# A hybrid attention and convolution layer on one core: the differences of the weight blocks on GpSimd from pair 23 of the first half on, and two more low halves on VectorE

## The chip, the cores and the metric

The kernel runs on one core of one Trainium2 chip. The core has five engines with queues of their own: TensorE (PE; its weight loads are PEld), VectorE (DVE), ScalarE (ACT), GpSimd (POOL) and SyncE (SP), which here only issues DMAs. Each engine does its queue in order and waits on semaphores for the others. The metric is the device time of one execution in microseconds.

## The reference

One layer with two token mixers, for a prompt of 2048 tokens and for 8 sample tokens, all in float32 (D = 1024; the input projection has 8704 columns):

```python
mod = c @ w_c + b_c;  shift, scale, gate = split(mod, 3)
z = (x * (1 + scale) + shift) @ w_in + b_in
q, k, v, ga, glu, gb, ma, mb = split(z)
# A: dilated causal window attention, 3 groups x 4 heads, combined over the groups by softmax of lse
a = (o_attn * silu(ga)) @ w_pa
# B: GLU, causal depthwise conv of width 31, LayerNorm over channels, swish
b = (conv_out * silu(gb)) @ w_pb
y = (sigmoid(ma) * a + sigmoid(mb) * b) @ w_o
x_out = layer_norm(ALPHA * x + gate * y)
# sample tokens: the same, with attention over caches and a kept conv state
```

The change lies in the weights of `w_in`, in the product that gives `z`.

## The kernel before

**Tiles and stages.** A product in float32 accuracy is made of three passes of a reduced form (float32r): each operand X is split into a high part H, ScalarE's copy of X in that form, and a low part L = X - H, and H·H + L·H + H·L is summed in PSUM. The product with `w_in` goes over two halves of the tokens (`p` 0 and 1) and, in each, over 34 pairs of column blocks of 128 columns. A pair with its 2 x 2 blocks (two blocks of the sum index, `e`, by two column blocks, `x`) is done by Strassen's scheme in Winograd's form: seven products for eight, with the operands b11, b21, T2, T1, T3, b22, T4 from the weights, where T1 to T4 are differences of blocks. In the first half each of the seven goes over two sets of 258 columns, in the second over 512 at once. The function `quad(s, ...)` issues the seven products of pair `s` in a fixed order, into the PSUM banks X, Z, Y and W. Of those, W and Y are single: VectorE must have emptied a bank (`out_of`, line L80, into a staging tile `zst`) before the next product starts there; X and Z are emptied by ScalarE (L568, L579, L589).

**The weights.** `w_raw` loads blocks into tiles `raw` and `rawb` (128 partitions x 512 numbers, 256 KB) over SP's queue. `w_make(s, n)` makes operand `n` of pair `s`. Its `split(r)` takes one of seven buffers `bop`, has ScalarE copy the high part (L238) and GpSimd or VectorE subtract for the low part (L247); a counter gives two of seven low halves to VectorE, by its steps T1 and T4. In the first half the differences are made too: `sub` (L76 on VectorE) makes T1's block with b21, T2's block (`t`) and T4's block with T2, and T3's block with T1; each of them is stored to DRAM (`tw_d`) for the second half, which only loads and splits them. `MAKE` says at which of a pair's 14 steps each operand is made: six products ahead of its first use, b11 and b21 at steps 8 and 9 of the pair before, T2 at 11, T1 at 13, then T3, b22 and T4 at 0, 3 and 5.

**What sets the order.** Everything is issued by one program in the order of the text; each engine's queue is the order of issue. Between products `tick()` lets lanes of other work go on: attention, convolution, normalisation (`conv_norm`), the sample attention (`s_attn`) and the preparation of the second half (`prep_second`). It keeps a planner's clock for TensorE and one for VectorE: every operation on VectorE adds its cost to `clock["dve"]` by `cost`, about 0.68 us for 512 columns, and a lane goes on only while VectorE's clock is less than 0.5 us ahead of TensorE's. A low half on GpSimd is booked at 0.3 us. `later` puts off stores by 2.6 us of the planner's clock.

**Pairs 23 to 33** are the second pair of the convolution's gate, two pairs of the attention's gate and eight pairs of merge gates. While they run, the lanes do the sample attention (products of caches with a query on VectorE, `y<-y,stg`, each followed by a sum), the normalisation of the first half's convolution (statistics on VectorE, three small operations on `lnm` on GpSimd at L772, L773, L834, then ScalarE at L835) and the preparation of the second half. GpSimd also copies two columns of each staged tile (`samples_of`, L615).

Of the kernel before, what the change touches and what calls it, by code (L numbers as in the profile page):

```python
# [11 lines left out]
OP = mybir.AluOpType  # L12
# [29 lines left out]
def f32(ap):  # L42
    return ap.bitcast(F32)
# [3 lines left out]
def hybrid_layer(ctx: ExitStack, tc: tile.TileContext, I, O):  # L47
    nc = tc.nc
    ctx.enter_context(tc.manual_schedule())
    PE, ACT, DVE, POOL = nc.tensor, nc.scalar, nc.vector, nc.gpsimd  # L50

    def ld(out, in_):
        nc.sync.dma_start(out, in_)
# [5 lines left out]
    clock = {"pe": 0.0, "dve": 0.0, "conv": 0.0}  # L59

    def cost(ap, per=1.2, fix=70):
        n = 1
        for s in ap.shape[1:]:
            n *= s
        clock["dve"] += (fix + per * n) / 1000.0
# [8 lines left out]
    def vtt(out, a, b, op):  # L74
        cost(out)
        DVE.tensor_tensor(out, a, b, op=op)  # L76
# [15 lines left out]
    def later(fn, delay=2.6):  # L92

        post.append((clock["pe"] + delay, fn))
# [89 lines left out]
    stream = [(p, n) for p in range(2) for n in range(len(quads[p]))]  # L184
# [47 lines left out]
    split_no = [0]  # L232
    on_dve = [2]

    def w_make(s, n):
        def split(r):
            t = bops[s, n] = bp.tile([P, 2, 4, P], F32R, name="bop", tag="bop", bufs=nbop[0])
            ACT.activation(t[:, 0], r, AF.Copy)  # L238
            split_no[0] += on_dve[0]
            eng = POOL  # L240
            if split_no[0] >= 7:
                split_no[0] -= 7
                eng = DVE
                cost(r)
            else:
                clock["dve"] += 0.3
            eng.tensor_tensor(t[:, 1], r, f32(t[:, 0]), op=OP.subtract)  # L247

        if stream[s][0]:
            split(raws.pop((s, n)) if n[0] == "T" else raws.pop((s, int(n[1]) - 1, int(n[2]) - 1)))  # L250
            return

        def sub(out, a, b, keep):
            vtt(out, a, b, OP.subtract)
            later(lambda: ld(tw_d[stream[s][1], T_OF[keep]].rearrange("p (k n) -> p k n", n=P), out))

        R = lambda e, x: raws[s, e, x]
        if n == "b11":
            split(R(0, 0))
        elif n == "b21":  # L260
            split(R(1, 0))
            sub(R(0, 0), R(0, 1), R(0, 0), "T1")
        elif n == "T2":
            t2 = wp.tile([P, 4, P], F32, name="t2", tag="t2")
            sub(t2, R(1, 1), R(0, 0), "T2")
            split(t2)
            sub(R(1, 0), R(1, 0), t2, "T4")
        elif n == "T1":
            split(R(0, 0))
            sub(R(0, 1), R(1, 1), R(0, 1), "T3")  # L270
        elif n == "T3":
            split(R(0, 1))
        elif n == "b22":
            split(R(1, 1))
        else:
            split(R(1, 0))
            for k in [k for k in raws if k[0] == s]:
                raws.pop(k)
# [1253 lines left out]
    s = 0  # L1532
    for p in range(2):
        state["p"] = p
        cv = None
        for n, pair in enumerate(quads[p]):
            kind, a, b = pair[0]
# [305 lines left out]
```

## Time and profile before

| | us |
|---|---|
| median of 3 runs | 2201.32 (2198.42 to 2202.17) |
| the profiled execution | 2199.83 |
| its span | 2198.0 |
| TensorE busy | 2104.3 |
| VectorE busy | 1343.4 |
| GpSimd busy | 922.4 |
| ScalarE busy | 910.8 |

The first half of the tokens runs to about 925 us, the second from there to about 1780, and the output stage behind it. A view of lines or a timeline names the engine, the line of the code, the operation and its tiles as out<-in; an arrow in brackets names what ended the engine's wait just before. Times are microseconds from the span's start, the mean of one instruction in a group is in nanoseconds.

### The profile page before, as it was taken

How to read it: one execution, taken by the hardware profiler on the slowest of the kernel's cores; microseconds unless marked ns; L12 is line 12 of the kernel's file. 1: busy time of each engine (PE TensorE's matmuls, PEld its weight loads, DVE VectorE, ACT ScalarE, POOL GpSimd, SP SyncE). 2: the span in 40 equal slices, each digit the busy share in tenths (PEclk: the TensorE clock that was granted, in tenths of full speed). 3: DMA queues.
4: the chain of work that ended last, by engine and by line, in shares of the span. 5: the costliest groups of instructions: out<-in, count | busy, mean ns of one | idle time of the engine just before them, and what ended most of it. 6: DMA issues, size and time to landing. Idle time of an engine off the chain costs nothing.

```text
span 2198.0 us, 36412 instructions
## 1 busy us (share of the span) xinstructions
PE 2104.3 (96%) x13185; PEld 1859.5 (85%) x13185; DVE 1343.4 (61%) x2142; ACT 910.8 (41%) x2042; POOL 922.4 (42%) x943
## 2 busy tenths in 40 slices
PE   7799999999998899989999999999999988999998
PEld 3799999999998868968888888888888868888886
DVE  4667676777767733554676767634467826545455
ACT  3424444444444545534444444456555532111110
POOL 2455454444644432454444444445333446232332
PEclk9899999999999999999999999999999999999999
DMA  8265455556669765435554556567898866343320
GB/s 263 91 179 186 139 188 162 159 152 186 186 199 289 222 212 177 159 111 148 166 164 157 180 163 190 189 183 236 264 307 260 269 208 221 115 127 104 99 97 31
DMA packets 404046, 392.09 MB, mean 178 GB/s; under 512 B 26585, under 2 KB 331277, under 8 KB 402833
## 3 DMA queue, kind: packets, MB, share of 16 engines
q1 hardware_dynamic: 336277, 342.63, 50.4%
q10 hardware_dynamic: 67588, 47.13, 6.7%
q8 instruction: 104, 1.70, 0.3%
q14 instruction: 77, 0.63, 0.1%
HBM read 245.91 MB, written 144.29 MB: 178 GB/s over the span
## 4 chain that ended last, share of the span: by engine, by line
PE 52%; DVE 3%; DMA 2%; issue 2%; POOL 2%; ACT 1%; SPq 0%; POOLq 0%; DVEq 0%; ACTq 0%
PE ps_X L498 9%; PE ps_Z L498 9%; PE ps_W L498 9%; PE py L1783 7%; PE pab L1727 5%; PE ps_Y L498 5%; PE ps_S L1225 3%; PE ps_U L1265 1%; PE ps_S L1250 1%; DVE yL L76 1%; PE ps_S L653 1%; PE ps_U L1263 1%; DVE xr L80 1%; DVE st L1666 0%; DVE th L76 0%
## 5 line engine op out<-in xcount | busy, mean ns | idle before, releaser
L247 POOL TENSOR_TENSOR bop<-raw,bop 128x512 fp32r<-128x512 f32 x341 | 487.3, 1434 | 569.9 <-ACT bop L238 467.6
L498 PE MATMUL ps_W<-As,bop 128*128 128x258 f32 (+1 forms) x2448 | 437.6, 327 | 14.6 <-DVE zst L80 12.6
L498 PEld LDWEIGHTS ps_W<-As,bop 128*128 128x128 f32 x2448 | 359.8, 191 | 56.0 <-DVE zst L80 15.5
L80 DVE SCALAR_TENSOR_TENSOR y<-u,cwT,y 128x1024 f32<-128x1024 f32 x240 | 357.6, 1490 | 1.8
L238 ACT ACTIVATE bop<-raw 128x512 fp32r<-128x512 f32 x409 | 251.7, 624 | 77.4 <-DVE raw L76 26.4
L498 PE MATMUL ps_X<-As,bop 128*128 128x258 f32 (+1 forms) x1224 | 221.6, 328 | 10.0 <-ACT c L568 7.0
L498 PE MATMUL ps_Z<-As,bop 128*128 128x258 f32 (+1 forms) x1224 | 223.6, 328 | 2.2 <-ACT c L568 2.2
L498 PE MATMUL ps_X<-Aa,bop 128*128 128x258 f32 (+1 forms) x1224 | 219.0, 328 | 4.0 <-ACT bop L238 1.6
L498 PE MATMUL ps_Y<-Aa,bop 128*128 128x258 f32 (+1 forms) x1224 | 217.8, 325 | 0.6 <-POOL Aa L388 0.6
L498 PE MATMUL ps_Z<-Aa,bop 128*128 128x258 f32 (+1 forms) x1224 | 215.5, 324 | 0.0
L498 PEld LDWEIGHTS ps_X<-As,bop 128*128 128x128 f32 x1224 | 180.4, 192 | 30.0 <-ACT c L568 7.2
L498 PEld LDWEIGHTS ps_X<-Aa,bop 128*128 128x128 f32 x1224 | 182.3, 192 | 24.5 <-ACT bop L238 2.7
L498 PEld LDWEIGHTS ps_Z<-As,bop 128*128 128x128 f32 x1224 | 179.4, 190 | 22.0 <-ACT c L568 2.6
L498 PEld LDWEIGHTS ps_Z<-Aa,bop 128*128 128x128 f32 x1224 | 180.1, 190 | 17.5 <-issue 0.8
L498 PEld LDWEIGHTS ps_Y<-Aa,bop 128*128 128x128 f32 x1224 | 178.0, 189 | 19.1 <-issue 1.8
L1242 ACT ACTIVATE X<-X,mz 128x128 f32<-128x128 f32 (+1 forms) x192 | 87.0, 455 | 167.2 <-DVE mz L84 162.1
L80 DVE SCALAR_TENSOR_TENSOR zst<-ps_W,bT,c 128x258 f32<-128x258 f32 (+1 forms) x102 | 58.4, 573 | 133.7 <-ACT c L589 122.0
L247 DVE TENSOR_TENSOR bop<-raw,bop 128x512 fp32r<-128x512 f32 x68 | 51.9, 764 | 94.4 <-ACT bop L238 90.9
L80 DVE SCALAR_TENSOR_TENSOR X<-ps_S,tabh 128x512 f32<-128x512 f32 (+1 forms) x80 | 52.5, 657 | 81.9 <-PE ps_S L1225 75.6
L80 DVE SCALAR_TENSOR_TENSOR zst<-ps_Y,bT,c 128x258 f32<-128x258 f32 (+1 forms) x90 | 51.5, 572 | 79.3 <-PE ps_Y L498 55.2
L1680 ACT ACTIVATE xr<-xr,lnm 128x1024 f32<-128x1024 f32 (+1 forms) x16 | 19.9, 1244 | 184.0 <-POOL lnm L1679 184.0
L1727 PE MATMUL pab<-oH,wc0H 128*128 128x256 f32 (+1 forms) x256 | 74.3, 290 | 19.7 <-DVE ev L80 17.4
(312 smaller groups left out, 3792.4 us busy)
## 6 DMA issues: line engine op xcount, KB each, us to landing
raw<-w_in SPq DMA_DIRECT2D x205, 256.0 KB
raw<-tw_d SPq DMA_DIRECT2D x136, 256.0 KB
tw_d<-raw SPq DMA_DIRECT2D x102, 256.0 KB
tw_d<-t SPq DMA_DIRECT2D x34, 256.0 KB
rawb<-w_in SPq DMA_DIRECT2D x33, 256.0 KB
wc<-w_c SPq DMA_DIRECT2D x16, 512.0 KB
aq<-zq SPq DMA_DIRECT2D x16, 512.0 KB
xr<-x_prompt SPq DMA_DIRECT2D x16, 512.0 KB
```

The costliest lines, as they stand in the source:

```text
L76: DVE.tensor_tensor(out, a, b, op=op)
L80: DVE.scalar_tensor_tensor(out, a, s, b, op0=op0, op1=op1)
L238: ACT.activation(t[:, 0], r, AF.Copy)
L247: eng.tensor_tensor(t[:, 1], r, f32(t[:, 0]), op=OP.subtract)
L498: PE.matmul(acc[:, :n], w[:, i, b, :], a[:, b, off:off + n], start=start and b == 0 and x == 0, stop=b == 3 and x == 2, skip_group_check=True)
L653: PE.transpose(pt[:, i * P:(i + 1) * P], t[:, i * P:(i + 1) * P], ident)
L1225: PE.matmul(S[:, s:s + w, :], q_of(b), k_of(b, w), start=True, stop=True)
L1242: ACT.activation(X[:, s:s + w, :], X[:, s:s + w, :], AF.Exp, bias=mz[:, n, 0:1], accum_out=mz[:, n, 1:2])
L1250: PE.transpose(pt[:, s, :], X[:, s, :], ident)
L1263: PE.matmul(U[:, n, :], Y[:, s, :], v_of(b, 1), start=True, stop=False)
L1727: PE.matmul(p[:, :n], a, b[:, kt, :n], start=i == 0, stop=i == 11)
L1783: PE.matmul(py[h], a[:, d, c0:c0 + P], w[:, h * 512:(h + 1) * 512], start=f, stop=l)
```

## The change

From pair 23 on, in the first half alone, `sub` puts a difference on GpSimd and books 0.3 us of VectorE's clock for it, and the counter in `split` goes up by four instead of two, so that four of a pair's seven low halves go to VectorE. With the counter where it stands at pair 23 these are b21, T1, b22 and T4; b11, T2 and T3 stay on GpSimd.

```diff
@@ w_make / split
-            split_no[0] += on_dve[0]
+            split_no[0] += on_dve[0] + (2 if stream[s][0] == 0 and s >= 23 else 0)
             eng = POOL
             if split_no[0] >= 7:
                 split_no[0] -= 7
...
@@ w_make / sub
         def sub(out, a, b, keep):
-            vtt(out, a, b, OP.subtract)
+            if s < 23:
+                vtt(out, a, b, OP.subtract)
+            else:
+                clock["dve"] += 0.3
+                POOL.tensor_tensor(out, a, b, op=OP.subtract)
             later(lambda: ld(tw_d[stream[s][1], T_OF[keep]].rearrange("p (k n) -> p k n", n=P), out))
```

In numbers of instructions, 44 differences (four for each of 11 pairs) go from VectorE to GpSimd and 22 low halves from GpSimd to VectorE. Lines behind 258 stand four higher in the changed kernel.

VectorE's queue where pair 23's operands b21, T2, T1, T3 and b22 are made, before: `raw<-raw` is T1's difference, made with b21, `t_7897<-rawb,raw` and `raw<-raw,t_7897` are T2's and T4's, `raw<-rawb,raw` is T3's; `bop<-raw,bop` is a low half, `zst<-ps_...` the emptying of a bank.

```order
L80 SCALAR_TENSOR_TENSOR zst<-ps_W,bT,u_7688 128x258
L76 TENSOR_TENSOR raw<-raw 128x512
L80 SCALAR_TENSOR_TENSOR zst<-zst 128x256
L76 TENSOR_TENSOR t_7897<-rawb,raw 128x512
L76 TENSOR_TENSOR raw<-raw,t_7897 128x512
L80 SCALAR_TENSOR_TENSOR zst<-zst 128x256
L80 SCALAR_TENSOR_TENSOR zst<-ps_W,bT,c_7944 128x258
L247 TENSOR_TENSOR bop<-raw,bop 128x512
L76 TENSOR_TENSOR raw<-rawb,raw 128x512
L80 SCALAR_TENSOR_TENSOR zst<-zst 128x256
```

The same place of VectorE's queue in the changed kernel, up to b22's low half (`bop<-rawb,bop`):

```order
L80 SCALAR_TENSOR_TENSOR zst<-ps_W,bT,u_7688 128x258
L247 TENSOR_TENSOR bop<-raw,bop 128x512
L80 SCALAR_TENSOR_TENSOR zst<-zst 128x256 x2
L80 SCALAR_TENSOR_TENSOR zst<-ps_W,bT,c_7944 128x258
L247 TENSOR_TENSOR bop<-raw,bop 128x512
L80 SCALAR_TENSOR_TENSOR zst<-zst 128x256
L80 SCALAR_TENSOR_TENSOR ysS<-ysS,ps_S 128x8 x4
L80 SCALAR_TENSOR_TENSOR zst<-ps_Y,bT,c_7970 128x258
L80 SCALAR_TENSOR_TENSOR zst<-ps_W,bT,u_7877 128x258
L80 SCALAR_TENSOR_TENSOR zst<-zst 128x256
L247 TENSOR_TENSOR bop<-rawb,bop 128x512
```

b21's low half stands where the first difference stood; the two differences of T2's step and that of T1's step are gone from between the emptyings of W; b22's low half has come in three steps later.

GpSimd's queue for the same operands, before (`sgb<-zst` are the copied columns of staged tiles):

```order
L247 TENSOR_TENSOR bop<-raw,bop 128x512
L615 COPY sgb<-zst 128x2
L247 TENSOR_TENSOR bop<-raw,bop 128x512
L615 COPY sgb<-zst 128x2
L247 TENSOR_TENSOR bop<-t_7897,bop 128x512
L615 COPY sgb<-zst 128x2
L247 TENSOR_TENSOR bop<-raw,bop 128x512
L615 COPY sgb<-zst 128x2 x2
L247 TENSOR_TENSOR bop<-rawb,bop 128x512
```

And in the changed kernel, where the differences have the line L258:

```order
L247 TENSOR_TENSOR bop<-raw,bop 128x512
L619 COPY sgb<-zst 128x2
L258 TENSOR_TENSOR raw<-raw 128x512
L619 COPY sgb<-zst 128x2
L258 TENSOR_TENSOR t_7897<-rawb,raw 128x512
L247 TENSOR_TENSOR bop<-t_7897,bop 128x512
L258 TENSOR_TENSOR raw<-raw,t_7897 128x512
L619 COPY sgb<-zst 128x2
L258 TENSOR_TENSOR raw<-rawb,raw 128x512
L247 TENSOR_TENSOR bop<-raw,bop 128x512
L619 COPY sgb<-zst 128x2 x5
```

T2's step is now three operations of 128 x 512 in a row on GpSimd, with T3's difference and low half behind them, and nothing of that size follows in the pair until T4 has been made and the next pair begins.

## Rows read from the trace of the kernel before

**Rows 1.** Page, first part: busy us (share of the span) and instructions by engine.
```profile
PE 2104.3 (96%) x13185; PEld 1859.5 (85%) x13185; DVE 1343.4 (61%) x2142; ACT 910.8 (41%) x2042; POOL 922.4 (42%) x943
```

**Rows 2.** Stretches: us, busy PE, PEld, DVE, ACT, POOL, then PEclk, DMA share, GB/s.
```profile
500.00:660.00 160.00, 160.00 (x1312) 158.37 (x1312) 107.89 (x162) 72.09 (x177) 77.85 (x97) 1.00 0.63 194
660.00:770.00 110.00, 98.06 (x759) 94.30 (x758) 84.56 (x149) 56.32 (x127) 48.56 (x71) 0.97 0.82 255
770.00:925.00 155.00, 151.26 (x1094) 130.28 (x1093) 60.66 (x116) 78.23 (x179) 49.90 (x84) 0.99 0.61 190
```

**Rows 3.** Waits of TensorE, 660 to 925: total us, times, longest.
```profile
PE ps_W L498 <- DVE zst L80: 7.1, 8, 2.6
PE ps_Z L498 <- ACT c L568: 2.2, 2, 1.3
```

**Rows 4.** Timeline of TensorE, rows behind a wait: start, us; in brackets the wait.
```profile
664.81 1.85 PE L498 MATMUL ps_W<-As,bop 128*128 128x258 f32 x12 [2.58 <-DVE zst L80]
...
700.59 1.70 PE L498 MATMUL ps_W<-As,bop 128*128 128x258 f32 x12 [1.03 <-DVE zst L80]
...
732.30 0.55 PE L896 MATMUL ps_S<-ident,y 128*128 128x128 f32 x3 [1.31 <-ACT y L835]
747.43 2.40 PE L498 MATMUL ps_W<-As,bop 128*128 128x258 f32 x12 [2.06 <-DVE zst L80]
...
781.05 0.31 PE L983 MATMUL ps_S<-ident,y 32*128 32x32 f32 x3 [1.55 <-DVE y L72]
781.75 2.57 PE L498 MATMUL ps_W<-As,bop 128*128 128x258 f32 x12 [0.39 <-DVE zst L80]
840.30 0.24 PE L1009 MATMUL ps_S<-ident,y 32*128 32x32 f32 x1 [1.34 <-DVE y L80]
```

**Rows 5.** Stretches around two standstills, for the granted clock (PEclk).
```profile
672.00:747.40 75.40, 67.96 (x543) 65.21 (x542) 61.67 (x112) 39.27 (x89) 33.57 (x50) 1.00 0.86 264
747.40:753.00 5.60, 5.57 (x33) 5.57 (x34) 3.98 (x7) 2.37 (x5) 2.04 (x4) 0.70 1.01 300
...
781.70:787.00 5.30, 5.10 (x29) 4.80 (x30) 1.85 (x7) 3.80 (x10) 3.23 (x11) 0.68 1.01 310
```

**Rows 6.** Timeline of VectorE at 664, 739 to 744 and 838.
```profile
664.27 0.49 DVE L80 SCALAR_TENSOR_TENSOR zst<-ps_W,bT,u 128x258 f32<-128x258 f32 x1 [4.44 <-DMA sb_d<-zst]
...
739.06 0.69 DVE L76 TENSOR_TENSOR raw<-raw 128x512 f32<-128x512 f32 x1 [2.47 <-POOL bop L247]
...
743.21 0.67 DVE L76 TENSOR_TENSOR t<-rawb,raw 128x512 f32<-128x512 f32 x1
...
743.97 0.69 DVE L76 TENSOR_TENSOR raw<-raw,t 128x512 f32<-128x512 f32 x1
...
838.18 0.69 DVE L76 TENSOR_TENSOR raw<-raw 128x512 f32<-128x512 f32 x1 [1.51 <-POOL bop L247]
```

**Rows 7.** Lines, 660 to 925: busy us, mean ns | idle before, what ended it.
```profile
L247 DVE TENSOR_TENSOR bop<-raw,bop 128x512 fp32r<-128x512 f32 x20 | 13.9, 694 | 47.3 <-ACT bop L238 47.3
...
L76 DVE TENSOR_TENSOR u<-u,y 128x256 f32<-128x256 f32 x16 | 11.1, 697 | 0.5
...
L76 DVE TENSOR_TENSOR raw<-raw 128x512 f32<-128x512 f32 x10 | 6.9, 688 | 7.5 <-POOL bop L247 7.5
...
L238 ACT ACTIVATE bop<-t 128x512 fp32r<-128x512 f32 x10 | 6.3, 631 | 6.3 <-DVE t L76 4.8 <-ACT smg L609 1.1 <-DVE raw L76 0.2
```

**Rows 8.** Timeline of GpSimd and VectorE at 711 and 765.
```profile
711.82 1.29 POOL L247 TENSOR_TENSOR bop<-raw,bop 128x512 fp32r<-128x512 f32 x1 [0.81 <-ACT bop L238]
711.92 1.47 DVE L76 TENSOR_TENSOR u<-u,y 128x256 f32<-128x256 f32 x1
...
765.88 0.42 DVE L76 TENSOR_TENSOR u<-u,y 128x256 f32<-128x256 f32 x1
```

**Rows 9.** Waits of SP's queue, 660 to 925.
```profile
SPq L53 <- DVE raw L76: 31.8, 11, 8.9
```

**Rows 10.** Lines, 660 to 925: ScalarE's normalisation.
```profile
L835 ACT ACTIVATE y<-ps_S,lnm 128x512 f32<-128x512 f32 x8 | 6.2, 776 | 4.2 <-POOL lnm L834 2.3 <-POOL lnm L772 0.7 <-ACT smg L609 0.6
```

## The prediction

> **What bounds the kernel now.** The first view is the page's busy table: TensorE works for 2104.3 of 2198.0 us [rows 1], so another engine's load matters only where TensorE stands still for it. The second is the table of stretches. The change touches the weight splits of the pairs 23 to 33, which are made between about 660 us (the first moved difference starts right behind the first row of [rows 6]) and the end of the first half, at 925. Before that stretch, from 500 to 660, TensorE is busy all the time although VectorE is busy for 67% of it. From 660 to 770 TensorE is busy for 98.06 of 110 us and VectorE for 77%; from 770 to 925 TensorE for 151.26 of 155 and VectorE for 39% [rows 2]. So some 15.7 us of standstill lie in the part that changes, 11.9 of them in the first 110 us, where the dot products of the sample attention, the gates and the convolution's normalisation share VectorE with the weights.
>
> The third view, the waits of TensorE in that part, says who ended them: 7.1 us went by before a product into bank W while VectorE had still to empty it, 2.2 us before a product into Z for ScalarE's copy of X or Z [rows 3]; the timeline names the large ones singly [rows 4]. Then there is the clock. The granted clock is at its upper level, 2.4 GHz (1.00), through 672 to 747.4 although that holds a standstill of 1.31 us at 732.30. It is a mix of both levels, 0.70 and 0.68 on the mean, in the 5.6 us from 747.4 and the 5.3 us from 781.7 [rows 5], right behind the standstills of 2.06 us and of 1.55 and 0.39 us together. Each such stretch loses 5.6 x 0.30 = 5.3 x 0.32 = 1.7 us.
>
> **What the change removes.** Per pair VectorE gives away four differences and takes two more low halves: b21 and b22, beside T1 and T4 that it had. In the order of its queue b21's low half takes the very place of b21's difference (the second row of both pieces of VectorE's order above), so there nothing is won but a wait that changes its name: the difference waited for GpSimd's split, 7.5 us in 10 [rows 7]; the low half will wait for ScalarE's copy, which is what ends GpSimd's split too. At 838.18 the difference came after a wait of 1.51 us [rows 6] and the standstill at 840.30 stands behind it; ScalarE's copy for b21 ends there at about the same time, so I leave those 1.34 us in. What really leaves the queue are T2's two differences in a row and T3's one; b22's low half is new, at a place with no difference before.
>
> Sum over 11 pairs: 44 differences at 0.69 us are 30.4 us (the timeline's 0.69 and 0.67 [rows 6]), 22 low halves at 13.9 / 20 = 0.69 us [rows 7] are 15.3; VectorE is relieved by 15 us, 6% of 265 us.
>
> What of it TensorE gets, standstill by standstill [rows 4]. At 664.81 nothing: VectorE itself stood 4.44 us for a store of a staging tile [rows 6], before the first changed instruction. At 747.43: between 743.21 and bank W's emptying VectorE ran T2's differences, 0.67 and 0.69 us [rows 6]; without them 2.06 becomes 0.7, worth 1.4. At 781.05 and 781.75: T3's difference, 0.69, stands ahead of the chain of the softmax; 1.55 becomes 0.9 and 0.39 goes, worth 1.0. At 700.59 the same 0.69 of 1.03 goes, worth 0.7. The remaining four of the eight standstills for bank W are 7.1 - 2.58 - 1.03 - 2.06 - 0.39 = 1.0 us together; I take half, 0.5. Sum 3.6 us. With them the two low stretches of the clock should go, since both standstills end below the 1.31 us that left the clock alone: 3.4 us.
>
> **What it adds.** GpSimd runs a difference in 1.29 us (its own split of the same size [rows 8]) against 0.69. Per pair GpSimd has five operations of this size now and seven then: 9.0 us for 6.5, in a pair of 265 / 11 = 24 us, with its load at 98 of 265 us now [rows 2]. So it does not become the bound by load. Every split is made six products, some 10 us at 1.70 each [rows 4], ahead of its use, and the split's chain (a difference, ScalarE's copy of 0.63 us [rows 7], a low half) is 3.2 us, so no product should wait for a weight. Who waits in the new order: ScalarE's copy of T2 and of T3's block stands behind a GpSimd difference, 0.6 us longer, 22 x 0.6 = 13 us at most, on an engine that is half idle [rows 2]; behind the copy stand its copies of the banks X and Z. That could cost from nothing to the whole 2.2 us over again [rows 3]; I take half, 1.1. The stores of the differences stand on SP's queue, which already waits 31.8 us for VectorE's differences [rows 9]; the loads and stores behind them will start 0.6 to 2 us later, and the weights' loads have a whole pair of lead, so I take nothing. GpSimd's three small operations of a normalisation now can stand behind more differences: ScalarE's normalisation waited for them 3.0 us in all over eight cases [rows 10], and one of these waits became the 1.31 us at 732.30 [rows 4]; I take one more of that size, 1.3. The planner books less for VectorE, so the sample attention and the normalisation come up to ten products sooner; the same work is done, and behind pair 33 the order is word for word what it was, so I take nothing for it but the scatter in the range.
>
> **The sum.** 3.6 + 3.4 - 1.1 - 1.3 = 4.6 us gained. The profiled execution took 2199.83 us, 1.8 us of it outside its span and 1.5 us under the median of the runs; taken off the median, 2201.32 becomes 2196.7.
>
> **The port.** At 711.82 GpSimd subtracts until 713.11, and VectorE's product of two tiles in SBUF, begun at 711.92, takes 1.47 us and ends 0.3 us behind it; undisturbed it takes 0.42 [rows 8]. Over the part, 16 of these took 0.697 us each [rows 7]: 16 x 0.28 = 4.4 us of blocking. The new order puts GpSimd's differences right beside VectorE's low halves for b21 and T1, 22 times. The Trainium skill, "SBUF — State Buffer", section "Who interferes with whom", says that a VectorE instruction with two SBUF inputs and a GpSimd instruction that reads SBUF exclude each other, the later one standing until the other is through; the row of 711.92 agrees with that. By that rule both the old differences and the new low halves pay, and GpSimd's longer hold speaks against the change.
>
> **Rivals.** First, the relief is eaten (no change). With 22 low halves meeting a GpSimd difference for half its length, 22 x 0.65 = 14 us, VectorE's 15 us are gone; GpSimd's seven operations for five raise the 4.4 us of blocking to 6.2. Then only half of the 3.6 us comes and one of two low clock stretches stays: 1.8 + 1.7 - 2.4 = 1.1 us gained, 2200.2. For it: the low halves that now go to VectorE were hardly disturbed (0.694 on the mean [rows 7]) because both engines wait for the same copies, which ends here. Against it: the places that cost most, 743 to 744 and 776, lose their VectorE work altogether.
>
> Second, GpSimd's queue becomes the late one (slower). At T2 it now runs difference, low half and difference, and at T3 another difference: four operations, 5.2 of 24 us, where it ran two. Of eight normalisations 8 x 5.2 / 24 = 1.7 fall there; one that stands behind two operations waits 2.6 us, and ScalarE, which does things in order, holds back its copy of X or Z. Now such waiting, 3.0 us in all, gave 1.31 us of standstill; 2.5 us would be one like 747.43, with the clock's 1.7 behind it: 1.7 x 4.2 = 7.1 us. With the first rival's small gain, 7.1 - 1.1 = 6.0 us lost, 2207.3. It decides from two such standstills on. For it: VectorE's statistics come without regard to GpSimd. Against it: GpSimd is idle for 60% of the part and catches up within a pair.
>
> **How the numbers follow.** A run of this kernel can tell about 0.2%, 4.4 us, from no change. My forecast, 2196.7, lies just beyond it: 0.45 for faster. The best case takes all of VectorE's own share, 7.1 - 2.58 + 1.55 + 1.34 = 7.4 us, and both clock stretches, 3.4, at no cost: 2190.5. The eaten relief and its neighbourhood has 0.38, the late GpSimd queue 0.17. The forecast's own range is 2190.5 to 2199; for eight in ten it must reach over the second case and up to the edge of the third: 2190.5 to 2206.
>
> **What would show it.** Right: TensorE's wait for VectorE before bank W falls from 7.1 us to about 4 in 660 to 925, no standstill of 2 us behind 670, the granted clock 1.00 from 672 on to 925, and the stretch before 925 ends 4 to 5 us sooner. Port rival: VectorE's low halves grow well over 0.69 us, those on `raw` to 1.0 or more, and its busy time hardly falls. GpSimd rival: ScalarE waits longer for `lnm` and for GpSimd's differences, and new standstills end with ScalarE. What would make me wrong altogether is a standstill of over 2 us at a place that has none now, brought by the sample work that comes at other times.

## The result, and the profile after

The changed kernel took 2213.71 us (median; 2211.65 to 2214.71) against 2200.99 for the kernel before: a ratio of 1.0058, 95% interval [1.0046, 1.0069]. It is slower by 12.7 us, where 4.6 us of gain were forecast, and it lies above the range. The profiled execution of after took 2214.71 us, its span is 2212.9.

The first part of the page of after, busy us and share of the span, answers to [rows 1]:

```profile
PE 2108.4 (95%) x13185; PEld 1865.7 (84%) x13185; DVE 1335.1 (60%) x2120; ACT 910.3 (41%) x2042; POOL 947.2 (43%) x965
```

TensorE's busy time has hardly moved (2104.3 before). Load went from VectorE (8 us less) to GpSimd (25 us more), as the change says. So the lost time is TensorE's standstill, and the stretches of after (columns as in [rows 2]) say where:

```profile
660.00:770.00 110.00, 87.65 (x656) 85.07 (x655) 75.61 (x135) 50.95 (x114) 53.41 (x75) 0.91 0.84 256
770.00:925.00 155.00, 148.91 (x1082) 127.52 (x1081) 59.29 (x103) 76.46 (x176) 61.80 (x93) 1.00 0.55 176
```

From 660 to 770 TensorE works 87.65 us, where it worked 98.06, though VectorE is busy for 9 us less there. The place where both kernels go on alike is found with a landmark: near the end of the first half stands a wait of 3.00 us for bank W that both kernels have. TensorE's timeline, first of before, then of after:

```profile
934.91 2.21 PE L498 MATMUL ps_W<-As,bop 128*128 128x258 f32 x12 [3.00 <-DVE zst L80]
```

```profile
948.38 2.52 PE L502 MATMUL ps_W<-As,bop 128*128 128x258 f32 x12 [3.00 <-DVE zst L80]
```

The same work ends 13.5 us later, so 13.5 of the 14.9 us between the two profiled spans lie ahead of it, and what follows gives nothing back. One stretch from 645 to that landmark, first of before, then of after:

```profile
645.00:934.80 289.80, 271.23 (x2031) 246.28 (x2029) 164.22 (x300) 146.76 (x334) 108.80 (x168) 0.98 0.68 212
```

```profile
645.00:948.30 303.30, 271.94 (x2029) 247.76 (x2027) 157.46 (x280) 147.05 (x336) 132.32 (x190) 0.97 0.65 203
```

TensorE stands still for 289.80 - 271.23 = 18.6 us before and for 303.30 - 271.94 = 31.4 us after: 12.8 of the 13.5 us are standstill, and only 0.7 more is work. Who ended it, after, 660 to 938 (total us, times, longest), answers to [rows 3]:

```profile
PE ps_W L502 <- DVE zst L80: 14.9, 7, 5.1
PE ps_S L900 <- ACT y L839: 9.5, 5, 2.5
PE ps_U L1004 <- POOL y L995: 2.7, 1, 2.7
```

The wait for bank W was to fall from 7.1 to about 4; it doubled. TensorE's timeline of after, the rows behind the larger waits, answers to [rows 4]:

```profile
667.02 2.95 PE L502 MATMUL ps_W<-As,bop 128*128 128x258 f32 x12 [5.06 <-DVE zst L80]
...
707.06 0.90 PE L900 MATMUL ps_S<-ident,y 128*128 128x128 f32 x3 [2.52 <-ACT y L839]
728.45 1.70 PE L502 MATMUL ps_W<-As,bop 128*128 128x258 f32 x12 [2.35 <-DVE zst L80]
735.60 0.55 PE L900 MATMUL ps_S<-ident,y 128*128 128x128 f32 x3 [2.46 <-ACT y L839]
758.62 1.66 PE L502 MATMUL ps_W<-As,bop 128*128 128x258 f32 x6 [4.11 <-DVE zst L80]
764.23 0.90 PE L900 MATMUL ps_S<-ident,y 128*128 128x128 f32 x3 [2.44 <-ACT y L839]
790.21 2.88 PE L1004 MATMUL ps_U<-y,y 128*32 128x512 f32 x6 [2.67 <-POOL y L995]
```

The standstills that the forecast wanted to close, at 747 and 781, are no longer there, nor is the one at 840 that it left as it was. In their place stand six of 2.35 to 4.11 us, and the one at 664.81 has grown from 2.58 to 5.06. The clock didn't recover either: in the 5.6 us behind the new standstill at 758.62 the granted clock is 0.50, the lower level, 1.2 GHz.

ScalarE says why the longest of the new ones came. Its waits for GpSimd's differences, after, 660 to 938:

```profile
ACT bop L238 <- POOL t L258: 17.4, 9, 6.1
ACT bop L238 <- POOL raw L258: 14.1, 7, 4.6
```

31.5 us, where in the kernel before it waited 9.1 + 4.8 = 13.9 us for VectorE's differences in the same stretch:

```profile
ACT bop L238 <- DVE raw L76: 9.1, 10, 1.1
...
ACT bop L238 <- DVE t L76: 4.8, 3, 2.2
```

The timeline of after from 749 to 759 shows one such wait and its way to TensorE:

```profile
749.51 1.54 DVE L247 TENSOR_TENSOR bop<-raw,bop 128x512 fp32r<-128x512 f32 x1 [1.52 <-ACT bop L238]
...
753.55 0.58 POOL L776 TENSOR_SCALAR lnm<-lnm 128x1 f32<-128x1 f32 x1 [3.04 <-DVE lnm L835]
...
754.21 0.57 POOL L777 TENSOR_TENSOR lnm<-lnm,mhalf 128x1 f32<-128x1 f32 x1
...
754.89 0.27 POOL L838 TENSOR_SCALAR lnm<-lnm 128x1 f32<-128x1 f32 x1
755.11 1.26 POOL L258 TENSOR_TENSOR t<-rawb,raw 128x512 f32<-128x512 f32 x1
...
756.41 0.63 ACT L238 ACTIVATE bop<-t 128x512 fp32r<-128x512 f32 x1 [6.14 <-POOL t L258]
756.94 0.76 ACT L839 ACTIVATE y<-ps_S,lnm 128x512 f32<-128x512 f32 x1
...
757.61 0.38 ACT L593 ACTIVATE c<-ps_Z 128x258 f32<-128x258 f32 x1
758.08 0.49 DVE L80 SCALAR_TENSOR_TENSOR zst<-ps_W,bT,c 128x258 f32<-128x258 f32 x1 [2.50 <-ACT c L593]
```

To be read from the bottom up: VectorE's emptying of bank W, for which TensorE waits 4.11 us, waits for ScalarE's copy `c` of bank Z; that stands in ScalarE's queue behind the copy of T2, which waits 6.14 us for T2's difference; and that stands in GpSimd's queue behind three small operations of a normalisation, which wait 3.04 us themselves for VectorE's statistics. The difference needs none of these; it only stands behind them. On VectorE, where it was before, it stood in another queue. The statistics are late in turn: VectorE works without a pause from 749.51 until they are through, and begins with b21's low half, which takes 1.54 us beside T1's difference on GpSimd (1.28 us from 749.22), where 0.69 is usual [rows 7].

### The profile page after: what moved, and what is told of

The parts are those of the page before. It is cut to its first block, busy times and chain, and to the rows that moved or that the text cites. A ratio compares the mean times of both kernels' runs of the same rounds, so it can differ in the third digit from the quotient of the medians.

```text
span 2212.9 us, 36391 instructions
## 1 busy us (share of the span) xinstructions
PE 2108.4 (95%) x13185; PEld 1865.7 (84%) x13185; DVE 1335.1 (60%) x2120; ACT 910.3 (41%) x2042; POOL 947.2 (43%) x965
## 4 chain that ended last, share of the span: by engine, by line
PE 79%; DVE 7%; DMA 4%; POOL 4%; issue 3%; ACT 2%; SPq 1%; ACTq 0%; POOLq 0%; DVEq 0%
PE ps_X L502 15%; PE ps_W L502 15%; PE ps_Z L502 15%; PE py L1787 8%; PE ps_Y L502 7%; PE ps_S L1229 5%; PE pab L1731 5%; PE ps_U L1269 2%; PE ps_S L1254 1%; PE ps_S L657 1%; PE ps_U L1267 1%; DMA stg<-smp_d 1%; DVE yL L76 1%; PE ps_U L1004 1%; POOL bop L247 1%
## 5 line engine op out<-in xcount | busy, mean ns | idle before, releaser
L247 POOL TENSOR_TENSOR bop<-raw,bop 128x512 fp32r<-128x512 f32 x330 | 470.5, 1431 | 541.4 <-ACT bop L238 433.8
L502 PEld LDWEIGHTS ps_Z<-Aa,bop 128*128 128x128 f32 x1224 | 180.2, 190 | 17.6 <-issue 0.8
L247 DVE TENSOR_TENSOR bop<-raw,bop 128x512 fp32r<-128x512 f32 x79 | 68.1, 863 | 94.3 <-ACT bop L238 79.2
L80 DVE SCALAR_TENSOR_TENSOR zst<-ps_W,bT,u 128x258 f32<-128x258 f32 (+1 forms) x102 | 58.2, 570 | 58.5 <-PE ps_W L502 40.5
```

What stands on the lines that cost most here:

```text
L80: DVE.scalar_tensor_tensor(out, a, s, b, op0=op0, op1=op1)
L502: PE.matmul(acc[:, :n], w[:, i, b, :], a[:, b, off:off + n], start=start and b == 0 and x == 0, stop=b == 3 and x == 2, skip_group_check=True)
```

## The experiments

All times are medians; the kernel before, run beside them, took 2200.3 to 2202.1 us in the four groups.

| run | what it is | us | ratio to before | 95% interval |
|---|---|---|---|---|
| before_again | the kernel before | 2200.63 | 1.0003 | 0.9994 to 1.0012 |
| e1 | differences moved, low halves not | 2211.74 | 1.0055 | 1.0039 to 1.0071 |
| e2 | low halves moved, differences not | 2201.03 | 1.0000 | 0.9991 to 1.0010 |
| e3 | the change, in the old order of work | 2205.44 | 1.0022 | 1.0011 to 1.0034 |
| e10 | the new order of work, old engines | 2201.76 | 0.9998 | 0.9989 to 1.0007 |
| e4 | T1, T4 on GpSimd; T2, T3 not | 2201.75 | 1.0005 | 0.9995 to 1.0015 |
| e5 | T2, T3 on GpSimd; T1, T4 not | 2208.86 | 1.0038 | 1.0023 to 1.0053 |
| e8 | the change, stores later | 2213.89 | 1.0063 | 1.0048 to 1.0078 |
| e9 | old order, stores later | 2203.70 | 1.0010 | 1.0000 to 1.0020 |
| e7 | the change, differences a step sooner | 2209.63 | 1.0040 | 1.0023 to 1.0056 |
| e13 | e7, stores later | 2210.56 | 1.0041 | 1.0029 to 1.0053 |
| e11 | e7 in the old order, stores later | 2205.20 | 1.0015 | 1.0006 to 1.0024 |
| e12 | T1, T4 on GpSimd, old order, stores later | 2203.52 | 1.0011 | 1.0000 to 1.0022 |
| e6 | the change from pair 29 on | 2201.81 | 1.0002 | 0.9993 to 1.0011 |

TensorE's and ScalarE's queues are those of before in e3, e9, e11 and e12, and those of after in e8 and e10. The others book differently, and each has an order of work of its own (e7 and e13 share one); what they show holds in that order.

### The scatter

The kernel before, once more as a run of its own. 

> The kernel before, once more, for a second profile. Same time within 0.2%. The standstill at 664.81, which a store of a staging tile ends ahead of the first moved instruction, is 2.58 us in the first profile and 5.06 in that of the changed kernel: if it is the change's, it is 2.6 here again; if it is the transfers' scatter, it may be anything from 2 to 5.

Measured 2200.63, ratio 1.0003. Its standstills lie within a microsecond of [rows 4] and have nearly the same sizes (2.76 for 2.58, 2.08 for 2.06).

### Which half of the exchange (e1, e2)

e1 leaves the low halves shared out as before:

```diff
-            split_no[0] += on_dve[0] + (2 if stream[s][0] == 0 and s >= 23 else 0)
+            split_no[0] += on_dve[0]
```

> The differences of pairs 23 to 33 on GpSimd, but two of seven low halves on VectorE as before. Theory (ScalarE stands behind GpSimd's differences for T2 and T3, and its copies of the banks with it): GpSimd has nine operations a pair instead of seven, so at least the changed kernel's loss, 12 us or more, and ScalarE's waits for GpSimd's differences at 30 us or more. Rival (the two further low halves on VectorE, which wait for ScalarE's copies and meet GpSimd on the port, are what costs): less than half of the loss, 6 us or less. Rival (the lanes come at another time because the planner books less): about the loss, since the booking of the differences is as in the changed kernel.

e2 leaves the differences on VectorE:

```diff
-            if s < 23:
-                vtt(out, a, b, OP.subtract)
-            else:
-                clock["dve"] += 0.3
-                POOL.tensor_tensor(out, a, b, op=OP.subtract)
+            vtt(out, a, b, OP.subtract)
```

> Four of seven low halves on VectorE from pair 23 on, the differences stay on VectorE. Theory (ScalarE behind GpSimd's differences): none of it is left, within 4 us of the kernel before, ScalarE's waits for differences at 14 us as before. Rival (low halves on VectorE): half of the loss or more, 6 to 12 us. VectorE has 22 operations more than before, so a loss of some us by its load alone is possible in either.

e1 is 10.9 us slower than before, e2 not at all. The differences bring nearly the whole loss. In e2 VectorE got 21 low halves, some 15 us of work, on top (43 for 22, 645 to 925), in the very stretch in which its load seemed to hold TensorE up, and it cost nothing that can be measured. TensorE's waits for bank W did grow, 660 to 925:

```profile
PE ps_W L498 <- DVE zst L80: 12.8, 7, 2.9
```

They were 7.1 us before [rows 3]; the other waits fell, in an order of work that is e2's own. So e2 shows that the time need not follow this one wait. That VectorE's load counts for nothing it doesn't show.

### Order or engines (e3, e10)

The change does two things at once: it puts operations on another engine, and, because the planner books 0.3 us for what it takes off VectorE, it brings the sample work and the normalisation up to ten products sooner. e3 keeps the bookings, and so the order of the other work, as before; TensorE's and ScalarE's queues are then those of before word for word:

```diff
-                cost(r)
+                if stream[s][0] == 0 and s >= 23 and n in ("b21", "b22"):
+                    clock["dve"] += 0.3
+                else:
+                    cost(r)
...
-                clock["dve"] += 0.3
+                cost(out)
                 POOL.tensor_tensor(out, a, b, op=OP.subtract)
```

> The changed kernel with the planner's clock booked as in the kernel before (0.68 us for a moved difference, 0.3 us for a further low half), so that TensorE's order and the lanes' places are those of the kernel before, word for word; only the engines of the 66 operations differ. Theory (ScalarE behind GpSimd's differences): most of the loss stays, 8 us or more. Rival (the loss comes from the lanes, which come sooner and so meet the weights at worse places): within 3 us of the kernel before.

e10 does the reverse: bookings, and so TensorE's and ScalarE's queues, of the changed kernel, and every operation on the engine that had it before:

```diff
-            split_no[0] += on_dve[0] + (2 if stream[s][0] == 0 and s >= 23 else 0)
+            split_no[0] += on_dve[0]
+            book_no[0] += on_dve[0] + (2 if stream[s][0] == 0 and s >= 23 else 0)
...
                 clock["dve"] += 0.3
-                POOL.tensor_tensor(out, a, b, op=OP.subtract)
+                DVE.tensor_tensor(out, a, b, op=OP.subtract)
```

> The engines as in the kernel before (all differences on VectorE, low halves shared out as then), but the planner books for the pairs 23 to 33 what the changed kernel books; so TensorE's and ScalarE's orders are those of the changed kernel word for word. With the order kept and the engines changed the loss was 4.6 us. If the order alone costs the rest of the 12.7: 2207 to 2210, 7 us or more over the kernel before, with standstills where the normalisation and the sample work now come. If order and engines cost only together (a normalisation's GpSimd operations in line right ahead of T2's difference, on GpSimd): 2199 to 2203, no loss, and no standstill above 2 us behind 670.

With the first row from before_again and the result above, this is a table of four:

| | old order | new order |
|---|---|---|
| old engines | 1.0003 | 0.9998 |
| new engines | 1.0022 | 1.0058 |

Neither e3's expectation of 8 us or more nor that of 3 or less was met; it lost 4.6. The order alone costs nothing, the engines alone 4.6 us, and both together 12.7: some 8 us come only where the two meet. ScalarE's waits for differences go the same way: 13.9 us before, 12.4 + 9.1 = 21.5 in e10, 31.5 in after, and in e3, 660 to 938, no more than before:

```profile
ACT bop L238 <- POOL raw L261: 8.1, 6, 2.1
ACT bop L238 <- POOL t L261: 6.4, 6, 1.5
```

So the moved differences make ScalarE wait longer only in the new order, and the 4.6 us of e3 are something else; it has 5.27 us of standstill at 667.20, for 2.58, and 2.46 at 844.83, for 1.34. e10's waits of TensorE, 645 to 930:

```profile
PE ps_S L904 <- ACT y L843: 8.7, 4, 3.3
PE ps_W L506 <- DVE zst L80: 6.2, 6, 2.7
```

The expectation that no standstill above 2 us would be left behind 670 was wrong: the new order by itself makes the standstills for the normalised tile `y`, 8.7 us, about the 9.5 of after, and closes others for it. So these are not GpSimd's doing. What the moved differences add in the new order is the rest: bank W 14.9 for 6.2, and `ps_U` 2.7 for 0.5. That is 8.7 + 2.2 us, and of them the 4.11 at 758.62 and the 2.67 at 790.21 are the largest; before the same products e10 waits 0.55 and 0.52 us. The latter, in after's timeline of GpSimd:

```profile
788.76 1.26 POOL L258 TENSOR_TENSOR raw<-raw,t 128x512 f32<-128x512 f32 x1
...
789.97 0.19 POOL L995 COPY y<-y 128x8 f32<-128x8 f32 x1
```

The small copies for which TensorE waits at 790.21 start right when a row of T2's difference, its low half and T4's difference is through. One operation of 0.19 us stands behind 1.26.

### Which differences (e4, e5)

e4 leaves T2's and T3's difference, behind which ScalarE copies at once, on VectorE:

```diff
-            if s < 23:
+            if s < 23 or keep in ("T2", "T3"):
```

> Only the differences T1 and T4, which no copy of ScalarE's waits for at once, are on GpSimd from pair 23 on; T2's and T3's stay on VectorE; the two more low halves are as in the change. Theory (the loss comes from ScalarE's copies that stand right behind GpSimd's differences for T2 and T3, and hold back its copies of the banks and its normalisation): at most 4 us over the kernel before, and that from the standstill near 667 us, which the store of T4's difference makes; ScalarE's wait for GpSimd's differences under 4 us, against 31.5 in the changed kernel. Rival (every moved difference costs alike, through the port or GpSimd's load): half of the change's loss, 5 to 8 us, and standstills all over the part.

e5 has `("T1", "T4")` in its place. 

> Only the differences T2 and T3, behind which ScalarE copies at once, are on GpSimd from pair 23 on; T1's and T4's stay on VectorE. Theory (ScalarE behind T2's and T3's differences): 8 us or more over the kernel before, ScalarE's wait for GpSimd's differences above 20 us, and standstills of 2 us or more that end with ScalarE's normalised tile or with bank W. Rival (all differences alike): 5 to 8 us over, as with the other two.

e4: 1.5 us over, within the scatter; e5: 8.6 us over. The times came as the theory said and not as the rival did. One number of e5's expectation failed: ScalarE's wait for GpSimd's differences was to be above 20 us, and there are 7.4 for T2's (8 times, longest 1.6). Its large standstills end with VectorE's emptying of W (3.14 at 728.90) and with ScalarE's small copy `smg` (3.56 at 781.30). Ahead of the latter ScalarE stands, up to 780.09, 3.75 us for VectorE's part of the sample attention's softmax, and not for a difference. So T2's and T3's are the dear pair in these two kernels, but each has an order of work of its own, and how much of the price is the order's is not shown. In the old order this pair costs nothing that can be measured: e9, with all four on GpSimd, is at 1.0010, and e12, with T1's and T4's alone, at 1.0011.

### A step sooner (e7)

Here T2's difference is made with b21 and T3's with T2, so that it is done when ScalarE comes to copy it:

```diff
         elif n == "b21":
             split(R(1, 0))
             sub(R(0, 0), R(0, 1), R(0, 0), "T1")
+            if s >= 23:
+                t2s[s] = wp.tile([P, 4, P], F32, name="t2", tag="t2")
+                sub(t2s[s], R(1, 1), R(0, 0), "T2")
...
             split(t2)
+            if s >= 23:
+                sub(R(0, 1), R(1, 1), R(0, 1), "T3")
             sub(R(1, 0), R(1, 0), t2, "T4")
```

> The changed kernel, but from pair 23 on T2's difference is made one step sooner (with b21), T3's with T2, still on GpSimd, so that a copy of ScalarE's no longer stands right behind the difference it reads. If ScalarE's wait for these differences is what the changed kernel loses behind 670: that wait falls from 31.5 to under 8 us, the standstills near 707, 728, 758 and 764 go, and the time falls to 2203 to 2206 (the one at 667 stays). If GpSimd's load or the port is the cause, the wait only moves and the time stays at 2211 to 2214.

2209.63: 4.1 us under the changed kernel, between the two expectations. ScalarE's waits for differences did go, 660 to 938, but others came:

```profile
ACT bop L238 <- POOL t L258: 8.1, 6, 1.9
ACT y L848 <- POOL lnm L847: 8.1, 5, 3.6
```

In after ScalarE waited only 0.9 us for `lnm` (660 to 925). Now the normalisation's small operations stand behind the differences, where the differences stood behind them.

The standstill at 758 fell from 4.11 to 1.24. But the one at 728 grew to 3.81, at 732.23, and 790 stayed (2.81 at 790.23). So making these differences sooner gives back about 4 of the 12.7 us (the intervals of e7 and after still overlap), and the rest stays.

### SP's queue (e8, e9, e13)

The first moved difference is T1's of pair 23, at 639.75 in after, not at 664 as I had it. The stores of these differences stand in SP's queue. SP's timeline, first before, then after:

```profile
644.17 0.39 SPq L53 DMA_DIRECT2D tw_d<-raw  x1
...
658.43 1.01 SPq L53 DMA_DIRECT2D sb_d<-zst  x2
```

```profile
646.63 0.32 SPq L53 DMA_DIRECT2D tw_d<-raw  x1
...
660.38 1.54 SPq L53 DMA_DIRECT2D sb_d<-zst  x2
```

T4's store waits for GpSimd and goes out 2.5 us later, and the staging stores `sb_d` behind it, for which VectorE stood 4.44 us at 664 [rows 6], are still 2 us late at 660. e8 puts the stores further behind:

```diff
-            later(lambda: ld(tw_d[stream[s][1], T_OF[keep]].rearrange("p (k n) -> p k n", n=P), out))
+            later(lambda: ld(tw_d[stream[s][1], T_OF[keep]].rearrange("p (k n) -> p k n", n=P), out), 2.6 if s < 23 else 6.0)
```

> The changed kernel with one number altered: from pair 23 on the stores of the differences go into SP's queue 6.0 us of booked TensorE time behind the difference, not 2.6, so that they find it done and hold nothing back. Every other engine's order is as in the changed kernel. Theory on the first standstill (SP stands on a store for GpSimd's difference, the weights' loads, the staging stores and the sample loads behind it come some 2.4 us late): the standstill at 667 goes from 5.1 (wait) and 2.95 (idle) back to about 2.6, and the time falls by 2 to 4 us, to about 2210.5; the standstills between 700 and 800 stay. Rival (the standstill comes from the port, which stretches VectorE's low half at 640 to 1.58 us): no change, 2213.

e9 does the same to e3, e13 to e7. 

> The change with the order of the other work held as in the kernel before (the planner's bookings unchanged), and with the stores of the differences 6.0 us of booked TensorE time behind them. If the loss of the change is the sum of the order (8 us) and of SP's queue (4.6), nothing is left: 2199 to 2203, the same as the kernel before. If SP's queue isn't it: 2205, as with the order kept and the stores at their old place.

> The changed kernel with the differences one step sooner (2209.6 by itself) and their stores 6.0 us behind (2213.9 by itself, though its first standstill was back at 3.0). If SP's hold and ScalarE's waits are what is lost and each hid the other: 2204 to 2207. If what remains is VectorE stretched by GpSimd's row of differences (port), and the normalisation behind that row: 2208 to 2211, with standstills near 732 and 790 as they are with the differences one step sooner alone.

The mechanism is shown: e8's first standstill is back at 3.02. TensorE's timeline of e8:

```profile
664.59 2.51 PE L502 MATMUL ps_W<-As,bop 128*128 128x258 f32 x12 [3.02 <-DVE zst L80]
689.37 1.71 PE L502 MATMUL ps_W<-As,bop 128*128 128x258 f32 x12 [1.72 <-DVE zst L80]
```

Its worth is not: e8 takes 2213.89 us, as long as the changed kernel. Some of the 2 us came back at once as the 1.72 at 689.37, where after waits 0.43 at 690.27; e13 gains nothing over e7. In the old order the later stores gave 1.7 us (e3 2205.44, e9 2203.70), within the two intervals. So SP's hold makes the standstill, but taking it away wins no time that can be told from none.

e13 has neither ScalarE's long waits for differences (8.2 us in all) nor SP's hold, though ScalarE waits 8.0 us for `lnm`, and still loses 9.5 us. Its timeline of VectorE and GpSimd ahead of its largest standstill:

```profile
725.62 1.29 POOL L247 TENSOR_TENSOR bop<-t,bop 128x512 fp32r<-128x512 f32 x1 [1.07 <-ACT bop L238]
725.66 1.52 DVE L76 TENSOR_TENSOR u<-u,y 128x256 f32<-128x256 f32 x1
726.86 1.45 POOL L258 TENSOR_TENSOR raw<-rawb,raw 128x512 f32<-128x512 f32 x1
727.11 1.49 DVE L80 SCALAR_TENSOR_TENSOR zst<-zst 128x256 f32<-128x256 f32 x1
728.27 1.44 POOL L258 TENSOR_TENSOR raw<-raw,t 128x512 f32<-128x512 f32 x1
728.52 0.68 DVE L843 BATCH_NORM_STATS2 ln<-ps_S 128x6 f32<-128x512 f32 x1
...
731.24 0.48 DVE L80 SCALAR_TENSOR_TENSOR zst<-ps_W,bT,c 128x258 f32<-128x258 f32 x1
```

```profile
731.77 2.95 PE L511 MATMUL ps_W<-As,bop 128*128 128x258 f32 x12 [4.21 <-DVE zst L80]
```

VectorE's first two operations, 0.42 us each when alone (`u<-u,y` [rows 8]), end 0.3 us behind the GpSimd operation beside which they started, and take 1.5. GpSimd had a row of three such operations in line, the low half at 725.62 and T3's and T4's differences; VectorE lost (1.52 - 0.42) + (1.49 - 0.42) = 2.2 us in it, ahead of bank W's emptying, about half of the 4.21. The remaining time up to 731.24 it works on statistics, staged tiles and the sample attention, without a pause.

### All remedies, and the cheapest part (e11, e12)

e11 is e7 with the bookings of the kernel before and the stores later. 

> All the remedies at once: differences on GpSimd one step sooner, the order of the other work as in the kernel before (TensorE's and ScalarE's rows are the same word for word), stores 6.0 us behind. If the three causes are all there is, and VectorE's relief is worth what the prediction gave it (3.6 us and the clock): 2195 to 2199, faster than the kernel before. If nothing is to be had from VectorE in this part: 2199 to 2203. If GpSimd's operations cost through the port all the same: 2203 or more.

e12 is e9 with T2's and T3's differences back on VectorE, by the same line as e4. 

> Only T1's and T4's differences on GpSimd, for the two low halves, order as in the kernel before, stores 6.0 us behind. No copy of ScalarE's waits for a moved difference, and SP is not held. VectorE's T2 and T3 differences stay at their places, so the standstill at 747 stays: 2198 to 2202, the same as the kernel before. If the port (GpSimd's differences beside VectorE's low halves of b21) costs: 2203 or more.

e11 loses 3 us, 1.0015 [1.0006, 1.0024]; e12, 1.0011 [1.0000, 1.0022], is at the edge of what can be told from no loss. No version beats the kernel before. One place where they lose is the one that I had left out of the sum, the standstill of 1.34 us at 840.30 [rows 4]. VectorE's timeline of e12 there, and TensorE's:

```profile
839.46 1.75 DVE L250 TENSOR_TENSOR bop<-raw,bop 128x512 fp32r<-128x512 f32 x1 [1.57 <-ACT bop L238]
...
841.13 1.45 DVE L80 SCALAR_TENSOR_TENSOR y<-ps_U,y 32x128 f32<-32x128 f32 x4
```

```profile
842.64 0.24 PE L1016 MATMUL ps_S<-ident,y 32*128 32x32 f32 x1 [2.46 <-DVE y L80]
```

The low half of b21, in the place of b21's difference, takes 1.75 us, because T1's difference runs on GpSimd beside it (1.28 us from 839.38); the difference took 0.69 [rows 6]. The standstill grew by 1.12 us. e3, e9, e11 and e6 have it too, at 2.46 to 2.47; e6 shows that by itself it is too little to be measured.

### Only the later pairs (e6)

```diff
-            split_no[0] += on_dve[0] + (2 if stream[s][0] == 0 and s >= 23 else 0)
+            split_no[0] += on_dve[0] + (2 if stream[s][0] == 0 and s >= 29 else 0)
...
-            if s < 23:
+            if s < 29:
```

> The change from pair 29 on, from about 815 us, where VectorE is busy for 39% and the kernel before has one standstill of 1.34 us left. If the loss needs the neighbourhood of the sample work and the normalisation (660 to 800): 2199 to 2203, no change. If each pair costs alike: 5/11 of 12.7, 2206 to 2208.

2201.81, no change. So nearly all of the loss belongs to pairs 23 to 28, where the dot products and the normalisation share VectorE, ScalarE and GpSimd with the weights.

## Why the prediction was wrong

**What held.** Which stretch it would be decided in; that VectorE's work for T2 goes from the place ahead of 747; that the low halves for b21 would stand beside GpSimd's differences; and, among the rivals, half of the second's mechanism, an in-order GpSimd queue behind which ScalarE stands and holds back its copy of a bank. The other half was the wrong way round: it had the normalisation behind the differences, while ScalarE's waits for `lnm` fell from 3.0 us [rows 10] to 0.9 and the differences stood behind the normalisation. I gave it 2207.3 and a chance of 0.17; the loss, 12.7 us, is twice its 6.0. The sign for being wrong altogether came too: TensorE waits 2.67 us at 790.21 for the sample attention's copies.

**VectorE's relief, 3.6 us: nothing in the time.** In the old order, where the standstills can be followed one by one, those that I named did shrink. In e9 the 2.06 us at 747.43 became 0.78, where I had 0.7, and the 1.55 at 781.05 went:

```profile
753.12 1.71 PE L505 MATMUL ps_W<-As,bop 128*128 128x258 f32 x12 [0.78 <-DVE zst L80]
```

But bank W's waits together did not fall: they are 8.3 us in e9 for 7.1, and products into Z wait 1.36 and 1.37 us for ScalarE's copies `u`, at 718.86 and 746.31, where before they did not. So the step failed in counting a shorter row on VectorE as time of TensorE's, standstill by standstill, as if nothing else became late instead. In the new order even the place is gone: at 758.62 VectorE itself waits 2.50 us for ScalarE's copy `c`, while ahead of 747.43 in before it worked without a pause from 739.06 on.

**The clock, 3.4 us: nothing,** since new standstills took the place of the old; TensorE's busy time to the landmark grew by 0.7 us.

**ScalarE's copies behind differences, 1.1 us: about 4** (e7). The step counted what a difference takes longer, 0.6 us. ScalarE's waits for differences grew by 17.6 us, more than the 13 us that I had as the most. What counts is what stands ahead of a difference in the new queue: the wait at 756.41 is 6.14 us, of which the difference itself is 1.26.

**The order of the other work, nothing: right by itself (e10), wrong in this change.** This is the largest step. It was costed alone, as was GpSimd's queue; together they cost 8 us more than apart. In the new order a normalisation stands ahead of T2's difference, and the copies for `ps_U` behind T4's.

**GpSimd's normalisation, 1.3 us: no cost of GpSimd's.** The standstills for the normalised tile rose to 9.5 us, but e10 has 8.7 of them with the old engines and is not slower.

**SP's queue, nothing: half right.** I argued with the weights' loads, which do have a pair of lead. The staging stores behind the same stores have none. The standstill of 2.58 that I left as it was, because it stood ahead of the first changed instruction, was behind it: the change starts at 640, and it grew to 5.06. e8 takes that back and wins no time.

**The port.** The first rival priced it at 0.65 us for each of 22 low halves. The rows, VectorE's low halves on `raw`, 645 to 925, first of after, then of e2 (the same low halves, no moved difference):

```profile
L247 DVE TENSOR_TENSOR bop<-raw,bop 128x512 fp32r<-128x512 f32 x30 | 28.4, 945 | 45.6 <-ACT bop L238 41.0 <-POOL y L996 1.6 <-DMA stg<-smp_d 1.4
```

```profile
L247 DVE TENSOR_TENSOR bop<-raw,bop 128x512 fp32r<-128x512 f32 x32 | 22.1, 691 | 42.5 <-ACT bop L238 41.0 <-DMA stg<-smp_d 1.5
```

30 x (0.945 - 0.691) = 7.6 us, half of the 14 that I took. Of this `u<-u,y` gives some back: 16 at 0.465 us for 0.697 [rows 7], 3.7 us, about half of it by the order alone (0.582 in e10). T1's and T4's differences alone make the low halves 0.801 us (e4), T2's and T3's alone 0.736 (e5). VectorE's load in all fell by 8 us, not by 15. The rule of the Trainium skill, "SBUF — State Buffer", section "Who interferes with whom", that an operation of VectorE with two inputs in SBUF and one of GpSimd that reads SBUF exclude each other, agrees with the rows of e12 and e13 above (1.75 us for 0.69, 1.52 and 1.49 for 0.42).

**What stays open.** The shares don't add up cleanly: ScalarE's shorter waits for differences are worth about 4 us (e7), and 9.5 us of loss are left in e13, of which the rows show the port (2.2 us at 731) and GpSimd's row of operations (2.80 at 789.58), and 2.45 us at 763 for a copy of ScalarE's. No run took the port away and left the queue, or the reverse, so how they share that rest is not shown; the low half at 749.51 in after, stretched ahead of the statistics for which GpSimd waits, suggests that the one feeds the other. Nor is it shown why e5's loss passes through other waits than after's.

## What to carry to other kernels

Before an operation is moved to an idle engine, read what will stand ahead of it in that engine's queue and who stands behind its reader: an idle share of 60% says nothing of a wait of 6 us behind a normalisation that waits itself. A standstill that ends with an engine is that engine's load only if the engine is not waiting too, and a shorter one is time won only if nothing else is late right behind it (e9). Where a change alters a planner's bookings as well as an engine, run the two apart before judging either, since here each alone cost 0 or 5 us and the two together 13.

## What the hardware showed that I had not expected

That the stretching passes on: two operations of 0.42 us, each beside another GpSimd operation of a row, took 1.52 and 1.49 us one behind the other (e13, 725.66 and 727.11), because as soon as one is through, the next meets the following GpSimd operation. A row on GpSimd thus held VectorE to GpSimd's own pace for two operations with both inputs in SBUF, where I had priced collisions one by one. The statistics at 728.52, whose one input is in PSUM, took 0.68 us beside the third operation of the row, as they take with GpSimd idle (0.69 at 752.55 in after).
